# Block products for the mixer's projections, with their weight blocks prepared during the first gate/up

## The chip, the cores and the metric

The kernel runs on one core of a Trainium2 chip. The core has five engines that each take their own instructions in order: PE (TensorE, matmul), DVE (VectorE), ACT (ScalarE), POOL (GpSimd) and SP (SyncE), the last of which only issues transfers here. The metric is the time of the program on the device in microseconds, over one block of the network with T = 1024 tokens and D = 1024.

## The reference

One encoder block in float32, three residual steps with layer norms. FF is 4096, there are 8 attention heads of width 64, and the recurrent part has 512 channels.

```python
x = layer_norm(DN_ALPHA * x + 0.5 * swiglu(x, ffn1_w_gate, ffn1_w_up, ffn1_w_down), ln1_g, ln1_b)
z = x @ w_in                        # columns: q, k, v, lx, lg (512 each), 8 forget gates
fox = forgetting_attention(q, k, v, fg)
u = causal_depthwise_conv(lx, conv_w, conv_b)
lru = gelu(lg) * rg_lru(u, ...)     # h_t = a_t h_{t-1} + sqrt(1 - a_t^2) (i_t u_t)
x = layer_norm(DN_ALPHA * x + concat(fox, lru) @ w_out, ln2_g, ln2_b)
x = layer_norm(DN_ALPHA * x + 0.5 * swiglu(x, ffn2_w_gate, ffn2_w_up, ffn2_w_down), ln3_g, ln3_b)
# swiglu(x, wg, wu, wd) = (silu(x @ wg) * (x @ wu)) @ wd
```

## The kernel before

**Precision.** Every float32 product is three matmuls in the format fp32r (`mm3`, L163 to L165): each operand is split into a high part (a cast on ACT) and a low part (a subtraction on DVE), and high x high, low x high and high x low are accumulated.

**Stages.** The kernel goes through gate/up 1 (to about 630 us), down 1 (to 919), the mixer's projections (to about 1183), the attention and W_out (to about 1370), gate/up 2 (to 1985) and down 2. At each seam the next stage's first operands need DVE and ACT.

**Block products.** gate/up and down multiply 2 x 2 block matrices with seven block products instead of eight (Strassen's scheme). In gate/up each of 16 pairs of column groups has two matrices, gate and up, and for each the products `one, two, six, five, seven, three, four` of 12 matmuls of 128x512. Their weights are sums and differences of four blocks of the weight, called 11, t1, 22, t2, 21, t4, t3. Normally DVE forms and splits these as it goes (L344 and others); the copies and additions of the products' results are done by ACT and DVE between.

**Prepared weights.** For the first pair of gate/up 2 these seven operands are made ahead, during gate/up 1. `prepare` is a generator: at each step it casts, splits and stores one block of weights (`keep`, L277, L278, store to the DRAM tile `pre_d` at L282), with a difference (`less`, L285) between. The blocks come over SP into two buffers called `aux`. A quarter job is one half of the rows of one matrix: six loads of 128 KB, seven keeps of 256 KB, four differences. There are four of them (2 matrices x 2 halves), 28 keeps in all. In gate/up 1 one step is taken for each matrix of pairs 1 to 15, behind product `two`. What the loop leaves over is drained by a bare loop after it. The keeps take their buffers from the pool `gu_ws`, whose space down 1 uses again for its own splits.

**Projections.** Before the mixer, x1 (the output of the first norm) is transposed and split into `xT`. For each of four groups of 128 columns, lx and lg, then q and k, are plain products: 8 blocks of x by 8 of w for each half of the tokens, 4 x 24 = 96 matmuls of 128x512 for two matrices. Their weights are loaded (`columns`) and split (`split_ws`) on the way. After groups 1 and 3 come eight tiles of v each (matmuls of 128x256). Convolution, gates and recurrence (`lru`) follow each half of lx and lg on ACT, DVE and POOL. q, k and v go to DRAM through POOL, and the attention loads them for each head over SP (`q`, `kh`, `kl`, `cum`, `v`).

**Order.** A scheduler orders each engine's instructions at build time, from the order of the code and from what each instruction waits for. `issue_after` keeps an instruction behind another one. On the chip each engine then takes its list strictly in order.

Of the kernel before, what the change touches and what calls it, by code (L numbers as in the profile page):

```python
# [9 lines left out]
F32 = mybir.dt.float32  # L10
# [7 lines left out]
P = 128  # L18
# [34 lines left out]
OPERANDS = "11", "t1", "22", "t2", "21", "t4", "t3"  # L53

# [5 lines left out]
class Block:  # L60
# [115 lines left out]
    def to_xT(self, i, in_s):  # L176

        nc = self.nc
        cols = slice((i % 4) * P, (i % 4 + 1) * P)
# [6 lines left out]
        self.scale_acc(i)  # L186
# [33 lines left out]
    def down_tile(self, i, f_tiles, scale, halves=(0, 1)):  # L220

        ts = slice(i * P, (i + 1) * P)
        for d in halves:
# [4 lines left out]
            self.nc.vector.scalar_tensor_tensor(self.acc[i][:, ds], pa, scale, self.acc[i][:, ds], op0=ALU.mult, op1=ALU.add)  # L228

# [32 lines left out]
    def prepare(self, views, to_d, wsp, ap):  # L262

        nc, v = self.nc, self.nc.vector

        def raw():
            return ap.tile([P, 2, P], F32, tag="aux", name=self.nm("aux"))

        def load(view, k, c):
            t = raw()  # L270
            nc.sync.dma_start(t, view[:, k:k + 2, c * P:(c + 1) * P])
            return t

        def halves(src):
            t = wsp.tile([P, 4, P], F32R, tag="ws", name=self.nm("ws"))
            hi, lo = t[:, 0:2, :], t[:, 2:4, :]
            nc.scalar.copy(hi, src)  # L277
            v.tensor_tensor(lo, src, f32(hi), ALU.subtract)  # L278
            return t

        def keep(m, h, n, src):
            nc.gpsimd.dma_start(to_d[m, OPERANDS.index(n), h], f32(halves(src)))  # L282

# [3 lines left out]
        for m, view in enumerate(views):  # L287
            for h in range(2):
                up, down = 2 * h, 4 + 2 * h
                a, b = load(view, up, 0), load(view, up, 1)  # L290
                yield
                keep(m, h, "11", a)
                less(b, a)
                a = load(view, down, 1)
                yield
                keep(m, h, "t1", b)
                yield
                keep(m, h, "22", a)
                less(a, b)
                b = load(view, down, 0)  # L300
                yield
                keep(m, h, "t2", a)
                yield
                keep(m, h, "21", b)
                less(b, a)
                a = load(view, down, 1)
                yield
                keep(m, h, "t4", b)
                b = load(view, up, 1)
                yield  # L310
                less(a, b)
                keep(m, h, "t3", a)
# [15 lines left out]
    def gate_up(self, wg, wu, h_d, rows, bank, tp, wsp, raws=None, later=None, aside=None, ready=None, steps=None):  # L328
# [211 lines left out]
        def ready_pair(g, u):  # L540
# [7 lines left out]
            def fetch(n, m, to):  # L548
                for l in range(2):
                    nc.sync.dma_start(f32(to[l]).rearrange("p (h k) f -> p h k f", h=2),  # L550
                                      ready[both.index(m), OPERANDS.index(n)].rearrange("h p (l k) f -> l p h k f", l=2)[l])
# [125 lines left out]
        for pair in range(FF // P // 2):  # L677
# [39 lines left out]
            for m in (gate, up):  # L717
# [18 lines left out]
    def down_ffn(self, wd, h_d, ln, order, vp, wp, finish, src, hooks, tail, homes, after=None):  # L736
# [6 lines left out]
        with self.pool("dn_gb") as gp, self.pool("dn_b") as bp, self.pool("dn_t", 2) as tp:  # L743
# [55 lines left out]
            def norm(i):  # L799
                self.layer_norm(i)  # L800

# [116 lines left out]
    def lru(self, c, half, s, tp, mix, state, between):  # L918

        nc, v = self.nc, self.nc.vector  # L920

        def tmp(tag, shape=(P, H), dt=F32):
            return tp.tile(list(shape), dt, tag=tag, name=self.nm(tag))

        zx = tp.tile([P, H + LINE], F32, tag="zx", name=self.nm("zx"))[:, 0:H + 3]
        if half == 0:
            v.memset(zx[:, 0:3], 0.0)
        else:
            v.tensor_copy(zx[:, 0:3], state["z"])
        nc.scalar.copy(zx[:, 3:], s[:, 0, :])  # L930
        if half == 0:
            state["z"] = self.small.tile([P, 3], F32, tag="zc", name=self.nm("zc"))
            v.tensor_copy(state["z"], zx[:, H:H + 3])
# [6 lines left out]
        v.tensor_tensor(ul, u, f32(uh), ALU.subtract)  # L940
        g = tmp("g")
        nc.scalar.activation(g, s[:, 1, :], AF.Square)
        nc.gpsimd.tensor_scalar(g, g, 0.044715, 1.0, op0=ALU.mult, op1=ALU.add)
        v.tensor_tensor(g, g, s[:, 1, :], ALU.mult)
        nc.scalar.activation(g, g, AF.Tanh, scale=GELU_C)
        v.scalar_tensor_tensor(g, g, 1.0, s[:, 1, :], op0=ALU.add, op1=ALU.mult)
        between()
# [19 lines left out]
        if half == 0:  # L967
            state["h"] = self.small.tile([P, 1], F32, tag="hc", name=self.nm("hc"))
            v.tensor_copy(state["h"], e[:, H - 1:H])
        v.scalar_tensor_tensor(g, g, -0.5, e, op0=ALU.mult, op1=ALU.mult)  # L970
        hs = slice(half * H, (half + 1) * H)
        nc.scalar.copy(mix[0][:, hs], g)
        v.tensor_tensor(mix[1][:, hs], g, f32(mix[0][:, hs]), ALU.subtract)
# [23 lines left out]
    def columns(self, w_in, *offs):  # L997

        r = self.raw([P, 2, KT, P])
        for n, off in enumerate(offs):  # L1000
            self.nc.sync.dma_start(r[:, n], w_in.rearrange("(k p) f -> p k f", p=P)[:, :, off:off + P])
        return [self.split_ws(r[:, n], KT) for n in range(2)]

    def mixer_in(self, w_in, lw, qw, later):

        nc = self.nc
        wv = w_in.rearrange("(k p) f -> p k f", p=P)
        self.q_d, self.k_d = (self.dram.tile([HEADS // 2, 2, P, T], F32, name=f"{n}_d") for n in "qk")
        self.v_d = self.dram.tile([HEADS, T, P], F32, name="v_d")
        self.mix_lru = []  # L1010

        with self.tc.tile_pool(name="lru_t", bufs=1, reuse_waits="tile") as tp, \
                self.tc.tile_pool(name="lru_g", bufs=4, reuse_waits="tile") as gp, \
                self.tc.tile_pool(name="ev", bufs=3, reuse_waits="tile") as ev:
            def lru_half(c, half):
                s = self.s_tile()
                self.project(s[:, 0, :], lw[0], half)
                self.project(s[:, 1, :], lw[1], half)
                for g in later[:2]:
                    g()  # L1020
                self.lru(c, half, s, tp, mix, state, lambda: qk_half(c, half))

            def qk_half(c, half):
                s = self.s_tile()
                hs = slice(half * H, (half + 1) * H)
                for n in range(2):
                    self.project(s[:, n, :], qw[n], half)
                for g in later[2:]:
                    g()
                later.clear()  # L1030
                for n, (scale, dst) in enumerate(zip((-0.125, 1.0), (self.q_d, self.k_d))):
                    hl = [ev.tile([P, H], F32R, tag="ev", name=self.nm("ev")) for _ in range(2)]
                    nc.scalar.activation(hl[0], s[:, n, :], AF.Copy, scale=scale)
                    nc.vector.scalar_tensor_tensor(hl[1], s[:, n, :], scale, f32(hl[0]), op0=ALU.mult, op1=ALU.subtract)
                    for l in range(2):
                        nc.gpsimd.dma_start(dst[c, l, :, hs], f32(hl[l]))

            def v_tile(i):
# [3 lines left out]
                for k in range(KT):  # L1042
                    wh, wl = (w[:, k % 4, :] for w in vw[k // 4])
# [359 lines left out]
```

## Time and profile before

| what | value |
|---|---|
| median of 3 runs | 2316.66 us (2316.2 to 2316.94) |
| the profiled execution | 2315.55 us, span 2313.8 us, mean granted clock 0.998 |
| PE busy | 2295.7 us, 99% of the span |
| DVE busy | 1634.9 us, 71% |
| ACT busy | 1017.2 us, 44% |
| POOL busy | 214.2 us, 9% |
| DMA | 314.67 MB, mean 136 GB/s |

Times in the rows are microseconds unless marked ns. A group of instructions is told as line, engine, operation, result <- inputs, shape and count, then busy time and mean ns of one, then the engine's idle time ahead of them with what ended it. Matmuls overlap: one lasts 0.39 us, but the next starts after a fraction of that.

### The profile page before, as it was taken

To read this page: it belongs to the slowest core of one execution; us is meant where nothing else is said; L and a number is where in the kernel's file an instruction comes from. 1 tells how busy PE (TensorE), PEld (TensorE's weight loads), DVE (VectorE), ACT (ScalarE), POOL (GpSimd) and SP (SyncE) were. 2 spreads that over 40 slices of the span, in tenths; PEclk is the share of its full clock that TensorE was granted. 3 is DMA by queue.
4 is the path that set the end of the run, shared out by engine and by line. 5 is a ranking of instruction groups with operands and counts; after the bars stand their busy time and mean duration, and the time that the engine had idled before them with its cause. 6 is when DMAs were issued, how large, how long until landed. Compare 5 with 4: busy or idle time off the path is not lost.

```text
span 2313.8 us, 28429 instructions
## 1 busy us (share of the span) xinstructions
PE 2295.7 (99%) x10705; PEld 1912.3 (83%) x10705; DVE 1634.9 (71%) x2509; ACT 1017.2 (44%) x1611; POOL 214.2 (9%) x369
## 2 busy tenths in 40 slices
PE   9999999999999999999999999999999999999998
PEld 7888888888888888888898888888888888888887
DVE  8766666666577788866667999565656566577886
ACT  5444434344344345453556855333333333344341
POOL 0121010101000000111133200000000000000000
PEclk9999999999999999999999999999999999999999
DMA  4333333333375443132275834232323232564541
GB/s 150 135 115 139 110 135 112 137 107 141 117 272 209 146 146 108 60 101 101 96 222 130 256 117 145 91 124 91 120 86 119 87 119 87 202 245 162 183 144 73
DMA packets 190249, 314.67 MB, mean 136 GB/s; under 512 B 9424, under 2 KB 113168, under 8 KB 190112
## 3 DMA queue, kind: packets, MB, share of 16 engines
q1 hardware_dynamic: 164800, 226.55, 30.3%
q0 software_dynamic: 25312, 86.31, 9.5%
q8 instruction: 84, 1.38, 0.2%
q14 instruction: 53, 0.43, 0.1%
HBM read 222.61 MB, written 90.21 MB: 135 GB/s over the span
## 4 chain that ended last, share of the span: by engine, by line
PE 94%; DVE 3%; ACT 1%; issue 1%; DMA 0%; SPq 0%; DVEq 0%; ACTq 0%
PE x L163 10%; PE x L165 10%; PE x L164 10%; PE b L163 8%; PE b L164 8%; PE b L165 8%; PE s L165 6%; PE s L164 6%; PE s L163 6%; PE a L163 6%; PE a L164 6%; PE a L165 6%; PE a L1188 1%; PE a L1167 1%; PE a L1045 1%; PE a L1047 1%
## 5 line engine op out<-in xcount | busy, mean ns | idle before, releaser
L343 ACT CAST ws<-t 128x512 fp32r<-128x512 f32 x240 | 149.1, 623 | 387.7 <-PE b L164 265.2
L343 ACT CAST ws<-raw 128x512 fp32r<-128x512 f32 x180 | 111.9, 623 | 248.7 <-PE x L164 243.1
L344 DVE TENSOR_TENSOR ws<-raw,ws 128x512 fp32r<-128x512 f32 x180 | 123.9, 689 | 127.2 <-ACT ws L343 114.8
L344 DVE TENSOR_TENSOR ws<-t,ws 128x512 fp32r<-128x512 f32 x240 | 164.7, 687 | 63.1 <-ACT ws L343 61.2
L164 PE MATMUL a<-ws,ws 128*128 128x512 f32 x512 | 199.7, 390 | 0.2
L163 PE MATMUL a<-ws,ws 128*128 128x512 f32 x512 | 199.3, 390 | 0.4 <-ACT row L667 0.4
L163 PE MATMUL b<-As,ws 128*128 128x512 f32 x512 | 199.4, 389 | 0.2 <-ACT row L658 0.2
L164 PE MATMUL b<-As,ws 128*128 128x512 f32 x512 | 199.3, 389 | 0.0
L165 PE MATMUL b<-As,ws 128*128 128x512 f32 x512 | 199.2, 389 | 0.0
L165 PE MATMUL a<-ws,ws 128*128 128x512 f32 x512 | 199.2, 389 | 0.0
L163 PE MATMUL x<-As,ws 128*128 128x512 f32 x504 | 196.2, 389 | 0.0
L164 PE MATMUL x<-As,ws 128*128 128x512 f32 x504 | 196.1, 389 | 0.0
L165 PE MATMUL x<-As,ws 128*128 128x512 f32 x504 | 196.1, 389 | 0.0
L163 PE MATMUL x<-A,ws 128*128 128x512 f32 x496 | 193.3, 390 | 0.1
L165 PE MATMUL x<-A,ws 128*128 128x512 f32 x496 | 193.1, 389 | 0.0
L164 PE MATMUL x<-A,ws 128*128 128x512 f32 x496 | 193.0, 389 | 0.0
L768 ACT CAST ws<-raw 128x1024 fp32r<-128x1024 f32 x112 | 117.4, 1050 | 159.2 <-PE a L164 88.2
L771 DVE TENSOR_TENSOR ws<-raw,ws 128x1024 fp32r<-128x1024 f32 x112 | 136.7, 1221 | 50.9 <-ACT ws L768 50.3
L697 POOL DMA_DIRECT2D h_d<-row x96 | 68.8, 719 | 969.1 <-DVE row L691 964.6
L163 PE MATMUL s<-ws,ws 128*128 128x512 f32 x384 | 149.5, 389 | 0.0
L165 PE MATMUL s<-ws,ws 128*128 128x512 f32 x384 | 149.4, 389 | 0.0
L164 PE MATMUL s<-ws,ws 128*128 128x512 f32 x384 | 149.4, 389 | 0.0
(290 smaller groups left out, 5231.9 us busy)
## 6 DMA issues: line engine op xcount, KB each, us to landing
raw<-h_d SPq DMA_DIRECT2D x56, 1024.0 KB, 5.4
h_d<-row POOLq DMA_DIRECT2D x96, 512.0 KB, 3.4
wd<-in_ffn_w_down_dram SPq DMA_DIRECT2D x32, 1024.0 KB, 7.6
raw<-in_ffn_w_gate_dram SPq DMA_DIRECT2D x30, 1024.0 KB, 5.3
raw<-in_ffn_w_up_dram SPq DMA_DIRECT2D x30, 1024.0 KB, 5.3
h_d<-row POOLq DMA_DIRECT2D x32, 256.0 KB, 2.4
raw<-in_w_in_dram SPq DMA_DIRECT2D x16, 512.0 KB, 4.9
pre_d<-ws POOLq DMA_DIRECT2D x28, 256.0 KB, 2.6
```

The lines of the kernel that those rows point to most:

```text
L163: mm(out, ah, bh, start=first, stop=False, skip_group_check=goes_on)
L164: mm(out, ah, bl, start=False, stop=False, skip_group_check=goes_on)
L165: mm(out, al, bh, start=False, stop=last, skip_group_check=goes_on)
L343: nc.scalar.copy(hi, src)
L344: v.tensor_tensor(lo, src, f32(hi), ALU.subtract)
L697: nc.gpsimd.dma_start(d[:, 2 * n:2 * n + 2], t.rearrange("p (r t) -> p r t", r=2))
L768: cast = nc.scalar.copy(hi, src)
L771: self.mark = v.tensor_tensor(lo, src, f32(hi), ALU.subtract)
L1045: nc.tensor.matmul(pa[:, 0:width], xh, wh[:, 0:width], start=k == 0, stop=False)
L1047: nc.tensor.matmul(pa[:, 0:width], xl, wh[:, 0:width], start=False, stop=k == KT - 1)
L1167: nc.tensor.transpose(pa[:, (j % 4) * P:(j % 4 + 1) * P], p[:, j * P:(j + 1) * P], self.ident)
L1188: mm(pv[:, ps], vt[:, j, :], pts[h, qt][j // 4][l][:, j % 4, ps], start=j == 0 and l == 0, stop=j == last and l == 1)
```

## The change

lx with lg, and q with k, of each column group become one unit: the 2 x 2 block matrix of tokens by two column blocks, with seven products of 12 matmuls (84 instead of 96). The operands of x for it (`s1` to `s4`) are formed and split by DVE and ACT from x1's rows ahead of the units, and the first 16 tiles of work in the mixer are now the v tiles. Since x1's rows are overwritten by those sums, they are stored to DRAM (`x1_d`) and loaded again in the attention.

The weights' seven operands for the eight units, and v's split, are no longer made in the mixer: `prepare` makes them in gate/up 1 and keeps them in DRAM (`wq_d`, `wv_d`). Its list is now 16 single blocks for v, 16 quarter jobs for the units, and the four quarter jobs for gate/up 2, in this order. A step is taken three times for each matrix instead of once. The `aux` buffers become four and are filled ahead; `gu_ws` has 15 buffers instead of 16.

The core of the diff:

```diff
     def prepare(self, jobs, wsp, ap):
+        specs = iter([src for blocks, _ in jobs for src in blocks])
+        ready = []
+        def fetch():                       # the next block over SP into an aux buffer
+            src = next(specs, None)
+            if src is not None:
+                t = ap.tile([P, 2 * P], F32, tag="aux", name=self.nm("aux"))
+                t = t.rearrange("p (k f) -> p k f", f=src.shape[-1])
+                nc.sync.dma_start(t, src)
+                ready.append(t)
         def keep(to, src):
...
             nc.scalar.copy(hi, src)
             v.tensor_tensor(lo, src, f32(hi), ALU.subtract)
-            nc.gpsimd.dma_start(to_d[m, OPERANDS.index(n), h], f32(halves(src)))
+            nc.gpsimd.dma_start(to, f32(t).rearrange("p l k f -> p l (k f)"))
...
+        for _ in range(4):
+            fetch()
+        yield
+        for blocks, to in jobs:
+            if len(blocks) == 1:           # v
+                keep(to, ready[0])
+                drop()                     # and fetch the next
+                yield
+                continue
+            a, b = ready[0:2]
+            keep(to["11"], a)
+            less(b, a)
+            drop()
+            yield
+            keep(to["t1"], b)
+            yield
...
 # gate_up, for each matrix of pairs 1 to 15
                 for step in ("two", "six", "five", "seven", "three"):
                     getattr(m, step)()
-                    if steps and step == "two":
+                    if steps and step in ("two", "five", "three"):
                         with self.tc.issue_after(self.weight_load.ins):
                             next(steps, None)
...
 # the kernel's body
-            blk.pool("gu_ws", 16) as wsp, blk.pool("aux", 2) as ap, blk.banks() as bank, ExitStack() as inner:
+            blk.pool("gu_ws", 15) as wsp, blk.pool("aux", 4) as ap, blk.banks() as bank, ExitStack() as inner:
...
-        steps = blk.prepare(blk.gu_views(ffn2_w_gate[0], ffn2_w_up[0]), pre_d, wsp, ap)
+        jobs = blk.mixer_jobs(w_in[0])
+        for m, view in enumerate(blk.gu_views(ffn2_w_gate[0], ffn2_w_up[0])):
+            jobs += blk.quarter_jobs(view, (0, P), lambda n, h: pre_d[m, OPERANDS.index(n)][:, :, h])
+        steps = blk.prepare(jobs, wsp, ap)
         finish = blk.gate_up(ffn1_w_gate[0], ffn1_w_up[0], h_d[0], rows, bank, tp, wsp, raws, open_s4, lambda: blk.mixer_consts(
...
         for _ in steps:
             pass
...
 # the mixer: one unit (lx with lg, or q with k)
+            def product(x, name, new=True):
+                w = w_ops.pop(0)
+                fetch_w()                  # the operand three products ahead, from wq_d over SP
+                for k in range(4):
+                    self.mm3(x, (w[:, 0, k, :], w[:, 1, k, :]), x_op(name, k), new and k == 0, k == 3, not new)
+            def unit(c0, c1, c3, then):
...
+                product(total, "11")
+                nc.scalar.copy(c0, total)
+                two = self.a_tile()
+                product(two, "12")
+                v.tensor_tensor(c0, two, c0, ALU.add)
+                product(total, "s2", False)
+                nc.scalar.copy(c1, total)
+                product(z, "s1")
+                nc.scalar.copy(c3, z)
+                product(total, "s3", False)
+                v.tensor_tensor(c3, total, c3, ALU.add)
+                product(z, "s4", False)
+                v.tensor_tensor(c1, z, c1, ALU.add)
+                product(total, "22", False)
+                then[7](total)
```

Between these calls `unit` runs the work that hangs on a finished part: convolution, gates, the stores of q and k, the splits of `s4` in the first unit, W_out's rows in the last.

**DVE at the end of gate/up 1.** Before, its list goes from the last pair's weight splits (L344), the last step (L278) and the combinations after products two, seven and three of the last matrix (L651, L661, L664) straight on to the splits of down 1's first operands (L771):

```order
L664 TENSOR_TENSOR row_4822<-b_4973,row_4823 128x512
L344 TENSOR_TENSOR ws_4900<-t_4897,ws_4899 128x512
L278 TENSOR_TENSOR ws_4956<-aux_4664,ws_4956 128x256
L651 TENSOR_TENSOR row_4824<-b_5042,row_4825 128x512
L771 TENSOR_TENSOR ws_5168<-raw_5155,ws_5167 128x1024
L661 TENSOR_TENSOR row_4825<-x_5013,row_4824 128x512
L664 TENSOR_TENSOR row_4825<-b_5069,row_4823 128x512
L771 TENSOR_TENSOR ws_5172<-wd_5157,ws_5171 128x1024
```

After, with the line numbers moved (steps are L283 and L287, the combinations L693, L703 and L706, down 1's splits L813), the beginning and the end of what stands there:

```order
L703 TENSOR_TENSOR row_5179<-x_5384,row_5178 128x512
L287 TENSOR_TENSOR aux_5533<-aux_5533,aux_5526 128x256
L283 TENSOR_TENSOR ws_5555<-aux_5533,ws_5555 128x256
L283 TENSOR_TENSOR ws_5559<-aux_5535,ws_5559 128x256
L287 TENSOR_TENSOR aux_5535<-aux_5535,aux_5533 128x256
L706 TENSOR_TENSOR row_5179<-b_5447,row_5177 128x512
L283 TENSOR_TENSOR ws_5566<-aux_5535,ws_5566 128x256
L287 TENSOR_TENSOR aux_5542<-aux_5542,aux_5553 128x256
```

```order
L283 TENSOR_TENSOR ws_5916<-aux_5887,ws_5916 128x256
L287 TENSOR_TENSOR aux_5894<-aux_5894,aux_5905 128x256
L283 TENSOR_TENSOR ws_5921<-aux_5894,ws_5921 128x256
L813 TENSOR_TENSOR ws_5971<-raw_5958,ws_5970 128x1024
L813 TENSOR_TENSOR ws_5975<-wd_5960,ws_5974 128x1024
```

Between the two pieces stand only L283 and L287: from behind L706 to L813 there are 91 rows of steps, 58 of L283 and 33 of L287. With those among the last pair's own rows, 69 of L283 and 39 of L287 lie between the last L693 and the first L813. On ACT the casts of the same steps (L282) stand ahead of down 1's first cast (L810).

**SP at the beginning of the attention.** `raw` are W_out's rows for the heads, `q`, `kh`, `kl`, `cum` and `v` are head 0's operands. Before, these loads follow the last load of the projections' weights (v's second half, L1081):

```order
L1081 DMA raw_9168<-in_w_in_dram 128x8x256
L1106 DMA raw_9434<-in_w_out_dram 128x2x1024
L1106 DMA raw_9444<-in_w_out_dram 128x2x1024
L1106 DMA raw_11160<-in_w_out_dram 128x2x1024
L1127 DMA q_9471<-q_d 64x1024
L1128 DMA kh_9472<-k_d 64x1024
L1129 DMA kl_9473<-k_d 64x1024
```

After, they follow the last two operands of the last q/k unit, a row of x1, and two loads of W_out's rows:

```order
L1130 DMA wq_10201<-wq_d 128x1024
L1130 DMA wq_10216<-wq_d 128x1024
L1396 DMA row_10326<-x_d 128x1024
L1273 DMA raw_12030<-in_w_out_dram 128x2x1024
L1273 DMA raw_12166<-in_w_out_dram 128x2x1024
L1291 DMA q_10330<-q_d 64x1024
L1292 DMA kh_10331<-k_d 64x1024
L1293 DMA kl_10332<-k_d 64x1024
```

The v tiles, which in the order of before stand on PE between the last q/k products and the attention's first scores, are at the mixer's beginning now; between the last unit and the first scores PE has only pieces of W_out.

More of the change, by code (lines that the diff above doesn't have):

```diff
@@ L916, in gate_w, with conv @@
         return self.split(raw, [P, 2, P], tp, "gw")
-    def lru(self, c, half, s, tp, mix, state, between):
+    def conv(self, c, zx, tmp):
         nc, v = self.nc, self.nc.vector
[L922 to L933, printed above, removed]
         u = tmp("u")
@@ L1014, in mixer_in, with tmp, v_weights, v_tile @@
                 self.tc.tile_pool(name="ev", bufs=3, reuse_waits="tile") as ev:
[L1015 to L1038, printed above, removed]
+            def tmp(tag, shape=(P, H), dt=F32):
+                return tp.tile(list(shape), dt, tag=tag, name=self.nm(tag))
+            def v_weights(cc, k):
+                if cc == 0:
+                    return tuple(t[:, k % 4, :] for t in vw[k // 4])
+                return tuple(t[:, k, :] for t in v1)
+            def v_tile(cc, i):
                 pa = self.a_tile()
@@ new lines, in parts @@
+            def parts(name, j, src):
+                js = slice(j * P, (j + 1) * P)
+                for hi, lo, x in zip(*(t if isinstance(t, list) else [t] for t in ops[name]), (src[:, 0:2], src[:, 2:4]) if isinstance(ops[name][0], list) else (src,)):
+                    self.cast = nc.scalar.copy(hi[:, :, js], x)
+                    last = v.tensor_tensor(lo[:, :, js], x, f32(hi[:, :, js]), ALU.subtract)
+                    if name == "s1" and j == 0:
+                        self.rest = last
@@ new lines, in fetch_w @@
+            def fetch_w():
+                at = next(loads, None)
+                if at is not None:
+                    t = self.wsp.tile([P, 4 * VW], F32R, tag="ws", name=self.nm("wq"))[:, 0:8 * P]
+                    self.row_load = nc.sync.dma_start(f32(t), self.wq_d[at].rearrange("p l h f -> p (l h f)"))
+                    if at[0] == 0 and at[1] < 3:
+                        self.issue_behind(self.row_load, self.rest)
+                    w_ops.append(t.rearrange("p (l k f) -> p l k f", l=2, f=P))
```

384 lines of the change are left out of this document (260 added, 124 removed).

## The prediction

> **What bounds the kernel now.** I read the busy shares first, then the chain that ended last, the table of windows, and the groups by form. The first fence holds the page's line of busy times, its chain by engine, and windows (columns: length, busy time and count of PE, PE's weight loads, DVE, ACT, POOL, then granted clock, DMA share, GB/s): gate/up 1 at rest, its last 40 us, the first 10 us of down 1, the mixer's projections, the attention.
>
> ```profile
> PE 2295.7 (99%) x10705; PEld 1912.3 (83%) x10705; DVE 1634.9 (71%) x2509; ACT 1017.2 (44%) x1611; POOL 214.2 (9%) x369
> ...
> PE 94%; DVE 3%; ACT 1%; issue 1%; DMA 0%; SPq 0%; DVEq 0%; ACTq 0%
> 0.00:58.00 58.00, 53.97 (x273) 44.82 (x274) 48.55 (x80) 34.81 (x60) 0.69 (x6) 0.97 0.42 150
> 400.00:470.00 70.00, 70.00 (x310) 57.96 (x310) 47.16 (x73) 28.08 (x48) 7.67 (x12) 1.00 0.38 134
> 590.00:630.00 40.00, 40.00 (x178) 33.14 (x177) 18.63 (x26) 13.53 (x21) 3.29 (x5) 1.00 0.36 133
> 630.00:640.00 10.00, 9.55 (x43) 7.58 (x42) 7.64 (x9) 4.48 (x5) 0.92 (x2) 1.00 0.77 274
> 919.00:1183.00 264.00, 263.04 (x1362) 224.65 (x1361) 180.09 (x330) 124.86 (x197) 43.27 (x69) 1.00 0.34 107
> 1183.00:1370.00 187.00, 182.98 (x1121) 157.89 (x1120) 156.89 (x388) 126.27 (x289) 54.99 (x117) 1.00 0.60 173
> ```
>
> PE bounds every stage: it is never idle in 400 to 470 us and idle 0.96 us of 264 in the projections. A matmul taken away is therefore worth its whole slot, and any wait that reaches PE is paid in full. The next view, PE's timeline where gate/up 1 ends, gives the slot (starts 0.226 to 0.227 us apart; over the window, 70/310 = 0.226) and the price of that seam today: 0.84 us from 630.56 to 631.39.
>
> ```profile
> 629.65 0.39 PE L165 MATMUL x<-A,ws 128*128 128x512 f32 x1
> 629.88 0.39 PE L163 MATMUL x<-A,ws 128*128 128x512 f32 x1
> 630.10 0.39 PE L164 MATMUL x<-A,ws 128*128 128x512 f32 x1
> 630.33 0.39 PE L165 MATMUL x<-A,ws 128*128 128x512 f32 x1
> 630.56 0.39 PE L163 MATMUL a<-ws,ws 128*128 128x512 f32 x1
> 631.39 0.73 PE L163 MATMUL a<-ws,ws 128*128 128x512 f32 x2 [0.45 <-ACT row L667]
> ```
>
> **Step 1, PE's work.** For each of the eight units (lx with lg, and q with k, four column groups each) seven products of 12 matmuls replace 96 matmuls of 128x512: 12 fewer each, 96 in all, and the order of PE has exactly 96 rows fewer. 96 x 0.2267 = **-21.8 us**. Nothing else on PE changes in number.
>
> **Step 2, the steps left over at the end of gate/up 1.** Here I expect the change to be decided. The generator of steps grows from 4 quarter jobs of 7 steps to 20, with 16 single blocks of v ahead: 1 + 16 + 140 = 157 steps. The loop over pairs takes three for each matrix, 15 x 2 x 3 = 90. So 67 are issued by the bare loop behind gate/up, and DVE's and ACT's orders show them ahead of the first operands of down 1: behind the combination after product two of the last up (row 742) stand 110 rows of DVE before L813's first, 69 of them splits (L283), 39 differences (L287). DVE and ACT work in order, so PE cannot begin down 1 before these are through. The durations are those of the same operations before: cast, difference, split, and the loads and stores that go with them.
>
> ```profile
> L277 ACT CAST ws<-aux 128x256 fp32r<-128x256 f32 x28 | 11.4, 406 | 13.7 <-PE x L164 11.5 <-DVE aux L285 2.0
> L285 DVE TENSOR_TENSOR aux<-aux,aux 128x256 f32<-128x256 f32 x16 | 6.8, 424 | 11.0 <-DMA aux<-in_ffn_w_up_dram 6.5 <-DMA aux<-in_ffn_w_gate_dram 4.3
> L278 DVE TENSOR_TENSOR ws<-aux,ws 128x256 fp32r<-128x256 f32 x28 | 11.9, 425 | 18.3 <-ACT ws L277 18.3
> L771 DVE TENSOR_TENSOR ws<-raw,ws 128x1024 fp32r<-128x1024 f32 x112 | 136.7, 1221 | 50.9 <-ACT ws L768 50.3
> L768 ACT CAST ws<-raw 128x1024 fp32r<-128x1024 f32 x112 | 117.4, 1050 | 159.2 <-PE a L164 88.2 <-PE s L164 60.5 <-issue 5.2
> ...
> DMA to landing us min/median/max: 2.1/2.7/7.2
> pre_d<-ws POOLq DMA_DIRECT2D x28, 256.0 KB, 2.6
> ```
>
> Let E be the end of PE's work in gate/up 1; product two of the last up ends five products earlier, at E - 5 x 12 x 0.227 = E - 13.6. Three paces are possible for a job of 7 splits and 4 differences:
> - DVE alone: 11 x 0.425 = 4.7 us. That is a floor only, since the differences chain: each of the four differences waits for the one before, and its cast and split follow it.
> - The chain difference, cast, split (0.424 + 0.406 + 0.425 = 1.26), four times, and three more splits of which one or two come beside it: with the handoffs I estimate 6.5 us when every block has landed. The four buffers of 128x256 are refilled as they fall free, so some loads are waited for; by the landing times in the fence (2.1 to 2.7 us, and more under load) I make it 7.4 to 8.4 us.
> - The DMA: a job loads 6 x 128 KB and stores 7 x 256 KB, 2.62 MB. From E - 13.6 on that is 69 stores and some 53 loads, 25 MB, and the first three 1 MB loads of down 1 fall among them: 28 MB. The busiest window above moved 274 GB/s at a share of 0.77, hence 356 at a full share: 79 to 103 us, of which the 15 buffers behind the stores take two jobs off DVE's shoulders.
>
> 9.86 jobs at 6.5 us are 64 us, at 8.4 us 83, by the DMA 79 to 103. Then come the landing of a last store that holds a buffer of down 1 (2.6, partly beside), one cast (1.05) and two splits of 1.22 before PE starts, some 3.7 us. I take 84 us for the jobs, near the upper chain and the lower DMA price since both press there: PE starts again at E - 13.6 + 84 + 3.7 = **E + 74**; the ends are E + 54 and E + 93. The Trainium skill, DMA: Bandwidth & Descriptors, Specifications, puts the HBM side at about 358 GB/s for a core; the trace's 0.77 share of 274 agrees, and by the page's figure alone the 28 MB take an estimated 78 us, so the gap would be E + 69.
>
> What would hide it: nothing. PE's first work in down 1 is L163 on the operands of L813. The loads of down 1's third slot stand behind all loads of steps on SP, and add to the wait rather than cover it.
>
> **Step 3, the last pair.** The copies of products six and five on ACT and the additions seven and three on DVE stand among step rows; a bank that is read late holds the next product. At 0.41 us a row and one to four rows ahead this is 0 to 3 us; I take **+1.5**.
>
> **Step 4, the clock.** The first window above, with PE's start after idling in it, was granted 0.97: 0.03 x 58 = 1.7 us lost. A gap of 70 us should cost the same: **+1.7**. The Trainium skill, TensorE: Matmul & The Clock Gate, Part 1, says that after an idle window of about 3.4 us PE runs at half clock for the next one; half of 3.4 is an estimated 1.7 us, and the row agrees.
>
> **Step 5, the 90 steps in the loop** (more casts, splits and stores per pair). DVE is busy 47.16 of 70 us; six steps a pair bring some 4 us in each 38.1 (168 slots), against 0.8 before. It stays under 80%, and matmuls do not wait: **0**. If the cover goes, PE waits for a split of a weight block, at most 1 to 2 us a pair, which I leave to the range.
>
> **Step 6, the mixer.** The 16 v tiles now come first, while DVE does the last norms, the transposes' splits and the sums of x blocks; the fifth v tile wants its bank back about when DVE has finished norm 7. 0 to 8 us, **+3**. In the units DVE loses its weight splits of 128x1024 (20 x 1.22 = 24.4) and gains the combinations of products; the prepared blocks are fetched three products ahead (3 x 2.72 us). DVE was busy 180.09 of 264 us, so (180.09 - 24.4) / 4 = 39 for a column group, of which I put some 7 (v tiles, transposes) ahead of the units: 32 us beside 2 x 84 + 12 slots of PE, 40.8 us. 0 to 6 us, **+1.5**.
>
> **Step 7, the seam to the attention.** Before, head 0's q, kh and kl were issued from 1164.77 while PE still had v tiles, so they lay hidden:
>
> ```profile
> 1164.77 0.47 SPq L1127 DMA_DIRECT2D q<-q_d  x1
> ...
> 1168.52 1.53 SPq L1129 DMA_DIRECT2D kl<-k_d  x1
> 1177.36 0.62 PE L1146 MATMUL s<-kh,q 128*128 128x512 f32 x2
> q<-q_d SPq DMA_DIRECT2D x16, 256.0 KB, 6.0
> kl<-k_d SPq DMA_DIRECT2D x16, 256.0 KB, 7.0
> ```
>
> Now the v tiles are done long ago, and these loads stand on SP behind two 1 MB loads of w_out that wait for buffers which the last q/k unit and the last gating release. The last k half leaves PE two products before the end; its store and load (2.6 and 6 to 7 us) follow, and PE has about 5.7 us of W_out pieces to cover. 3 to 12 us, **+8**.
>
> **Sum:** -21.8 + 74 + 1.5 + 1.7 + 0 + 3 + 1.5 + 8 = +67.9. The profiled execution took 2315.55 us (span 2313.8 and 1.75 around it), 1.1 under the median of 2316.66. 2315.55 + 67.9 = 2383.4, I say **2383**. With all low ends (-21.8 + 54 + 1.7 + 3) it is +37, 2352; with all high ends (-21.8 + 93 + 3 + 1.7 + 8 + 6 + 12) +102, 2418.
>
> **Rivals.**
> - The steps are no bound, faster. If DVE got through the leftover rows without holding down 1 (they would have to be done, or stand behind L813), only steps 1, 6 and 7 would count: -21.8 + 12.5 to -21.8 + 3, 2297 to 2306. It decides if the leftovers cost under 21.8 - 4 = 18 us, that is under 0.3 us for each of 108 rows from E - 13.6 on. Against it: each takes 0.425 by the groups above, and DVE keeps its order. 4 in 100.
> - The chain alone: loads and stores keep up and a job takes 6.5 to 7 us. PE starts at E + 54 to E + 59, total 2352 to 2366. For it: the stores of before landed in 2.6 us beside full work. 25 in 100.
> - The DMA is the bound and every load is late: 95 us or more for the jobs, E + 85 and beyond, total 2395 to 2420. For it: stores now write 1 KB runs, and 512-byte reads run beside them. 20 in 100. The Trainium skill, SBUF — State Buffer, SBUF: two separate sides, warns that certain DVE operations keep GpSimd from writing descriptors; if differences of two SBUF tiles did so, stores would be late and this case would hold.
> - The gain is not realised in the mixer, because DVE (32 of 40.8 us) and ACT evacuate late: 10 to 20 us on top, 2393 to 2403. 8 in 100.
> - No change within 0.2% (4.6 us, about what a measurement of this kernel can tell): several of these would have to cancel. 2 in 100.
>
> The forecast has the remaining 41. Slower in all cases but the first and the last: 94. The range 2350 to 2412 leaves out the faster case and the far ends.
>
> **What would show it.** In the changed profile: one idle stretch of PE of about 74 us at about 630, ended by DVE at L813, with DVE at L283 and L287 and ACT at L282 through all of it; DMA at 240 to 300 GB/s there. 96 fewer matmuls; gate/up 1 otherwise as long as before; the projections about 20 us shorter less some stalls; a gap before the first L1312. I am wrong if PE does not stop at 630, or stops under 20 us: then DVE ran these rows earlier than its order seems to allow, or in far less than 0.42 us each.

## The result, and the profile after

The changed kernel takes 2426.82 us (median of 4 runs, 2422.41 to 2433.25) against 2316.54: a ratio of 1.0478, 95% interval 1.0454 to 1.0502. It is slower by 110 us, where the forecast's sum was 67.9; the sign and the place were right, the size lies 15 us above the range. The profiled execution took 2425.57 us, its span is 2423.9.

The page of the changed kernel, its line of busy times and the chain; then windows, with the columns of the prediction's first fence: gate/up 1 at rest, its last 13 us, and the 86 us behind it.

```profile
PE 2290.4 (94%) x10609; PEld 1897.6 (78%) x10609; DVE 1720.0 (71%) x2745; ACT 1064.9 (44%) x1767; POOL 311.1 (13%) x505
...
PE 63%; DVE 2%; issue 2%; DMA 2%; ACT 2%; SPq 0%; POOL 0%; DVEq 0%; ACTq 0%; POOLq 0%
```

```profile
100.00:600.00 500.00, 495.74 (x2175) 408.64 (x2174) 351.76 (x591) 217.15 (x393) 98.73 (x147) 1.00 0.48 161
627.00:640.00 13.00, 11.72 (x52) 9.37 (x52) 7.38 (x19) 4.60 (x13) 6.78 (x10) 1.00 0.89 292
640.00:726.00 86.00, 1.01 (x5) 0.51 (x3) 38.53 (x93) 23.99 (x60) 41.17 (x60) 0.53 0.88 294
```

PE was 99% busy and is 94%: its busy sum is 5 us smaller, the span 110 us longer. In the last window it does nothing, DVE works less than half of the time (38.5 of 86 us), and the transfers are at a share of 0.88. PE's timeline shows both ends of that stop:

```profile
640.62 0.39 PE L167 MATMUL x<-A,ws 128*128 128x512 f32 x1
726.30 1.28 PE L165 MATMUL a<-ws,ws 128*128 128x512 f32 x2 [85.29 <-ACT ws L810]
```

From 640.62 to 726.30 are 85.7 us, for a distance of 0.23 before. Where the 110 us went, by the starts of the first and last matmuls of each stage in PE's timelines of the two kernels:

| stretch | before | after | difference |
|---|---|---|---|
| to the last matmul of gate/up 1 | 630.33 | 640.62 | +10.3 |
| from there to the first of down 1 | 0.23 | 85.68 | +85.5 |
| down 1 | 309.98 | 310.47 | +0.5 |
| mixer, to the last before the scores | 236.70 | 237.62 | +0.9 |
| from there to the first scores | 0.12 | 13.67 | +13.5 |
| attention, to the first product of gate/up 2 | 209.16 | 209.09 | -0.1 |
| the rest | 927.33 | 926.71 | -0.6 |

By these starts, down 1 of the kernel before ends at 940.5 us and its projections at 1177.2; the 919 and 1183 given with the stages above are rougher.

The mixer's +0.9 is -21.8 for the 96 matmuls, +5.4 for 24 matmuls of W_out that now stand ahead of the scores instead of behind them, and 17.3 us that are left over, most of them waits (shown below). The attention has those 24 fewer and is no shorter: it lost 5.3 us more. Some 2 of these are lost by the matmuls right behind the stop, up to ten of which start 0.43 us apart instead of 0.23, and 1.8 are more waits of PE; the remainder isn't traced.

These figures are from one profiled execution of each kernel. Where the same code ran in other runs below, gate/up 1 with 90 steps lost 8.0 to 10.6 us, and the stop ahead of the scores was 12.6 to 16.5 us.

The waits of all engines from 627 to 727 us (us in total, times, longest) and the landing times of the steps' loads there:

```profile
ACT ws L282 <- DVE aux L287: 45.4, 29, 5.7
DVE ws L283 <- ACT ws L282: 33.7, 53, 1.9
POOL wq_d L284 <- DVE ws L283: 31.4, 30, 5.4
DVE aux L287 <- DMA aux<-in_w_in_dram: 10.2, 6, 4.7
DVE ws L813 <- DMA pre_d<-ws: 1.5, 1, 1.5
```

```profile
DMA to landing us min/median/max: 2.2/3.7/7.2
```

Cast, split and difference wait for each other in a ring, as in the second pace of the forecast, and the ring waits for loads: 25 of the 55 were awaited, 30.3 us in all. Their median time to landing rose from 2.7 to 3.7 us; the longest is 7.2 as before. The last row is the store that holds down 1's buffer.

PE's own waits: two rows from gate/up 1, then the largest from the projections up to the scores:

```profile
PE b L165 <- ACT row L700: 3.6, 4, 2.2
PE x L165 <- DVE row L703: 1.3, 1, 1.3
```

```profile
PE s L1312 <- DMA kh<-k_d: 13.3, 1, 13.3
PE s L165 <- ACT raw L1157: 5.4, 8, 0.7
PE s L165 <- ACT raw L1160: 2.8, 4, 0.7
PE a L166 <- DVE w L158: 1.8, 2, 1.1
```

The twelve waits for L1157 and L1160 show on PE's timeline as a start 1.06 us after the last instead of 0.23:

```profile
1161.87 0.39 PE L167 MATMUL s<-As,wq 128*128 128x512 f32 x1
1162.93 0.50 PE L165 MATMUL s<-As,wq 128*128 128x512 f32 x1 [0.68 <-ACT raw L1157]
```

### The profile page after: what moved, and what is told of

Same layout as the page of the kernel before. It is cut to its first block, busy times and chain, and to the rows that moved or that the text cites. A ratio compares the mean times of both kernels' runs of the same rounds, so it can differ in the third digit from the quotient of the medians.

```text
span 2423.9 us, 29536 instructions
## 1 busy us (share of the span) xinstructions
PE 2290.4 (94%) x10609; PEld 1897.6 (78%) x10609; DVE 1720.0 (71%) x2745; ACT 1064.9 (44%) x1767; POOL 311.1 (13%) x505
## 4 chain that ended last, share of the span: by engine, by line
PE 63%; DVE 2%; issue 2%; DMA 2%; ACT 2%; SPq 0%; POOL 0%; DVEq 0%; ACTq 0%; POOLq 0%
PE a L166 6%; PE a L167 6%; PE a L165 6%; PE s L165 5%; PE x L167 5%; PE x L165 5%; PE x L166 5%; PE s L167 5%; PE s L166 5%; PE b L167 4%; PE b L166 4%; PE b L165 4%; PE a L1354 1%; DMA kh<-k_d 1%; PE a L1333 1%
## 5 line engine op out<-in xcount | busy, mean ns | idle before, releaser
L165 PE MATMUL a<-ws,ws 128*128 128x512 f32 x512 | 200.0, 391 | 85.3 <-ACT ws L810 85.3
L810 ACT CAST ws<-raw 128x1024 fp32r<-128x1024 f32 x112 | 117.5, 1050 | 163.5 <-PE a L166 83.0
L165 PEld LDWEIGHTS a<-ws,ws 128*128 128x128 f32 x512 | 96.5, 188 | 106.0 <-ACT ws L810 85.7
L813 DVE TENSOR_TENSOR ws<-raw,ws 128x1024 fp32r<-128x1024 f32 x112 | 136.6, 1220 | 51.4 <-ACT ws L810 49.5
L165 PE MATMUL s<-ws,ws 128*128 128x512 f32 x384 | 149.5, 389 | 0.0
L167 PE MATMUL s<-ws,ws 128*128 128x512 f32 x384 | 149.4, 389 | 0.0
```

The source lines that it names most:

```text
L165: mm(out, ah, bh, start=first, stop=False, skip_group_check=goes_on)
L167: mm(out, al, bh, start=False, stop=last, skip_group_check=goes_on)
L810: cast = nc.scalar.copy(hi, src)
L813: self.mark = v.tensor_tensor(lo, src, f32(hi), ALU.subtract)
```

## The experiments

Theory A is that of the forecast: the stop is the steps that the loop leaves over. The rivals were that the steps cost PE the same wherever they stand (B), and that down 1's own first loads set the stop (C). Inside the stop, the loads' waits (L) stood against the rate of the transfers (D). Runs without a ratio are single executions; since the changed kernel's own four executions lie 11 us apart, they are read by their stages and not by their totals.

### The steps spread over six places

```diff
                 m.one()
+                if steps:
+                    with self.tc.issue_after(self.weight_load.ins):
+                        next(steps, None)
...
-                    if steps and step in ("two", "five", "three"):
+                    if steps and step in ("two", "six", "five", "seven", "three"):
```

> The changed kernel with a step after each of six products of every matrix (one, two, six, five, seven, three: 180 places for 157 steps), so that nothing is left for the bare loop. Theory A (the stop of PE before down 1 is the leftover steps in the lists of DVE and ACT): the stop falls from 85.5 us to about 1, the stalls inside gate/up 1 grow with the steps from 10.3 to about 10.3 x 157/90 = 18, total 2425.6 - 84.5 + 7.7 = about 2349. Rival B (the steps need time that PE waits for wherever they stand, by DVE, ACT or the transfers): the stalls inside gate/up 1 grow by what the stop loses, total about 2400 to 2430.

Measured: 2352.41 us, ratio to before 1.0153 (1.0136 to 1.0170). PE's timeline at the seam, and PE's waits in gate/up 1:

```profile
657.50 0.39 PE L167 MATMUL x<-A,ws 128*128 128x512 f32 x1
657.73 0.39 PE L165 MATMUL a<-ws,ws 128*128 128x512 f32 x1
```

```profile
PE x L167 <- DVE ws L386: 6.2, 8, 1.7
PE x L165 <- ACT row L696: 3.7, 2, 2.1
PE x L165 <- ACT row L690: 2.7, 1, 2.7
```

The stop is gone whole, 85 us of it, so A holds, and B falls: where the stop lost 85 us, gate/up 1 grew by only 16.9. Still, it now ends at 657.5, 27.2 us later than before the change instead of the 18 expected: the cost in the loop grows faster than the number of steps.

### One step for each matrix

```diff
-                    if steps and step in ("two", "five", "three"):
+                    if steps and step == "two":
```

> The changed kernel with one step for each matrix, as before the change: 30 places, 127 steps left over instead of 67. Theory A at the 1.28 us that a leftover step cost (85.5/67): the stop grows by 60 x 1.28 = 77 to about 162 us, the stalls inside gate/up 1 fall from 10.3 to 1 or 2, total about 2493. Rival C (the stop is set by the first loads of down 1, which wait on SP's queue and for the transfers, not by the number of steps): it stays at some 85, total about 2417.

Measured: 2496.15 us, and on PE's timeline

```profile
792.06 1.28 PE L165 MATMUL a<-ws,ws 128*128 128x512 f32 x2 [159.61 <-ACT ws L810]
```

127 leftover steps stop PE for 160 us, 67 for 85.5: 1.26 and 1.28 us a step. The stop goes with the number of steps, so C falls. Gate/up 1 ends at 632.06, so 30 steps in the loop cost 1.7 us, 90 cost 10.3, 157 cost 27.2. This run has the same 15 weight buffers as the changed kernel, so the buffer taken away costs at most 1.7 us by itself.

### Eight buffers for the loads

```diff
-            blk.pool("gu_ws", 15) as wsp, blk.pool("aux", 4) as ap, ...
+            blk.pool("gu_ws", 13) as wsp, blk.pool("aux", 8) as ap, ...
...
-        for _ in range(4):
+        for _ in range(8):
             fetch()
```

> The changed kernel with eight aux buffers filled ahead instead of four (and 13 weight buffers instead of 15, to have the space). Theory L (a leftover job takes 9.8 us instead of the chain's 6.9 because its loads are awaited): jobs at about 6.9, 9.86 x 6.9 = 68 us from 13.6 before the end of gate/up 1, the stop falls to about 58, total about 2398. Rival D (28 MB at the 290 GB/s that the transfers move is the limit): the stop stays at 80 to 86, total 2420 to 2427.

Measured: 2414.05 us; PE's timeline, and the window of the stop:

```profile
711.81 1.28 PE L165 MATMUL a<-ws,ws 128*128 128x512 f32 x2 [71.59 <-ACT ws L810]
```

```profile
640.00:711.00 71.00, 0.22 (x1) 0.00 (x0) 35.67 (x93) 21.13 (x60) 41.11 (x59) 0.52 0.99 357
```

The stop shrinks from 85.3 to 71.6, between L and D. With loads further ahead the transfers run at a share of 0.99 and 357 GB/s, so for these bytes there is hardly more to gain: the 14 us were awaited loads, the 71.6 left are the bytes. The forecast had 356 GB/s for a full share, and its lower price by the transfers comes to E + 69 (79 - 13.6 + 3.7). The Trainium skill, DMA: Bandwidth & Descriptors, Specifications, gives about 358 GB/s for a core's HBM side; this window agrees.

A second thing: the loop's own loss is gone too. From 100 to 600 us, with the same 90 steps, PE makes as many matmuls as before the change (2207; the changed kernel 2175) and is never idle:

```profile
100.00:600.00 500.00, 500.00 (x2207) 413.81 (x2206) 356.02 (x601) 220.94 (x396) 98.76 (x147) 1.00 0.48 162
```

The two other executions with four buffers and 90 steps, in the next two experiments, made 2185 and 2187. So in the changed kernel the loss between these marks came from awaited loads. About 7 us came at the start instead (PE waits of 2.6 for L427 and 1.2 for L421); some 4 of them lie ahead of the first load of a step, at 52.65 us, so those belong to the 13 weight buffers and not to the loads.

### The second accumulator in its own tile

```diff
-                total, z = s[:, 0, :], s[:, 1, :]
+                total, z = s[:, 0, :], self.a_tile()
```

> The changed kernel with the unit's second accumulator z in a PSUM tile of its own instead of the second half of the tile that holds the first. Theory Z (PE's twelve waits of 0.83 us for ACT's copies L1157 and L1160 come from the two accumulators' sharing one tile, so that a product into one waits for the copy out of the other): the waits go, the projections are 10 us shorter, total about 2415. Rival: the copies are awaited for the products' own sake, or DVE's combinations are awaited instead: 0 to 3 us, total 2422 to 2426.

Measured: 2410.12 us. PE's waits from the v tiles to the scores:

```profile
PE s L1312 <- DMA kh<-k_d: 8.0, 1, 8.0
PE a L166 <- DVE ue L971: 2.0, 5, 0.8
PE a L165 <- ACT ua L970: 1.8, 4, 0.6
```

All twelve waits are gone and the projections are 10.2 us shorter (237.62 to 227.38). `total` and `z` were two halves of one tile, and a product into one half waited for the copy out of the other, though the data are apart. What was not expected: the wait at the scores fell too, from 13.3 to 8.0. Waits for the convolution (L970, L971), 3.8 us, have come up in their place.

### W_out's loads behind head 0's

```diff
-            self.nc.sync.dma_start(r, wv[:, f0:f0 + 2, :])
+            with self.tc.issue_after(self.row_load.ins):
+                self.nc.sync.dma_start(r, wv[:, f0:f0 + 2, :])
```

> The changed kernel with the two 1 MB loads of W_out's rows issued behind head 0's loads instead of ahead of them (nothing else). Theory S (PE's 13.4 us before the first scores are head 0's 128 and 256 KB loads queueing in the transfers behind those 2 MB): by the 5 to 7 us that 2 MB take at 290 to 360 GB/s the stop shrinks, to about 6 to 8 us, total about 2419. Rival (the loads wait for the last stores of q and k or for space, not for the transfers): the stop stays at 12 to 14, total 2422 to 2428.

Measured: 2415.26 us. The transfers that SP issues in the changed kernel, SP's longest wait there, then the transfers in this one, and PE's first scores in this one:

```profile
1270.01 1.77 SPq L1273 DMA_DIRECT2D raw<-in_w_out_dram  x2
1271.89 0.80 SPq L1291 DMA_DIRECT2D q<-q_d  x1
1272.79 0.55 SPq L1292 DMA_DIRECT2D kh<-k_d  x1
```

```profile
SPq L1273 <- DVE mix L1018: 16.7, 1, 16.7
```

```profile
1259.00 0.47 SPq L1292 DMA_DIRECT2D q<-q_d  x1
1261.34 0.45 SPq L1293 DMA_DIRECT2D kh<-k_d  x1
```

```profile
1271.94 0.40 PE L167 MATMUL a<-w,mix 128*128 128x512 f32 x1
1272.18 0.39 PE L1313 MATMUL s<-kh,q 128*128 128x512 f32 x1
```

The stop falls to nothing, more than theory S: it was not only the 2 MB in the transfers, but also SP's queue that held head 0's loads. Ahead of them stood two loads that wait for buffers, the first of them 16.7 us for the last gating (L1018). Without those two, q is issued 12.9 us earlier, 2 of them because the whole mixer runs that much earlier here. The rival falls. Of the 13.4 us the program kept some 8, since the attention became 5.5 us longer (214.66 against 209.09).

### The edits together, and what gate/up 1 still lost

First all of them, with six aux buffers and 14 weight buffers, or with eight and 13:

> The changed kernel with the steps in six places of every matrix, z in its own PSUM tile, W_out's loads behind head 0's, and six aux buffers with 14 weight buffers. By the sum of the single edits: 2352 (steps spread) - 15 (z; the stop before the attention shrank with it) - 6 (loads) = 2331; and if the 27 us of stalls inside gate/up 1 with spread steps come from loads of blocks that are awaited (four buffers), a part of them goes, some 10 us: about 2321. Rival (those stalls come from DVE's and ACT's lists being fuller, whatever the loads): gate/up 1 ends at 657 again, total about 2331. Faster than before only if nearly all of the 27 us go.

> As the one before with eight aux buffers and 13 weight buffers. With four places and eight buffers the stalls after 80 us had gone, and 7 us had come at the start (24 to 78 us). If awaited loads are the cause of the stalls of spread steps, gate/up 1 ends at about 640, total about 2314; if 13 weight buffers are too few for the weights' run ahead, stalls at the weights' splits grow and it is 2325 or more.

Measured: 2328.51 us, ratio 1.0045 (1.0031 to 1.0059), gate/up 1 ends at 648.9; and 2341.61, where it ends at 661.5. The first is 2.5 under the sum of single edits and 7.5 over the hope: six loads ahead took 8.6 of the 27 us, with one weight buffer fewer. The second, where gate/up 1 is 12.6 us longer again, falls to the other case of its expectation, that 13 weight buffers are too few: 7.1 us of these come in the first 80 us, as in the other run with 13. Whether the weight buffers or the eight loads cost the other 5.5 us is not separated.

Then each step was cut: cast now, split, difference and next load at the next step (here as a sketch of `keep`):

```diff
             nc.scalar.copy(hi, src)
-            v.tensor_tensor(lo, src, f32(hi), ALU.subtract)
-            nc.gpsimd.dma_start(to, ...)
+            def split():
+                v.tensor_tensor(lo, src, f32(hi), ALU.subtract)
+                nc.gpsimd.dma_start(to, ...)
+            later.append(split)            # run when the next step begins
```

> The kernel with all four edits (steps in six places, z in its own tile, W_out's loads behind head 0's, six aux buffers and 14 weight buffers), and each step cut in two: the cast stays where it was, the split, the difference and the next load move to the beginning of the following step, so that DVE does not wait in its list for the cast it has just asked for. Theory O (the 18.6 us that gate/up 1 still loses are DVE's and ACT's in-order lists waiting on each other inside a step, which makes the weight splits behind them late): most of it goes, gate/up 1 ends at 632 to 640, total 2310 to 2320. Rival F (DVE's list is simply fuller: 156 splits and 80 differences, 100 us, beside copies that PE awaits): gate/up 1 ends at 645 to 652 again, total 2324 to 2331.

Measured: 2322.95 us, ratio 1.0037 (1.0022 to 1.0051); gate/up 1 ends at 642.9. That lies between the two theories: 6.0 us of the 18.6 were the lists waiting inside a step, where theory O had hoped for most of them. Nearly half of the 12.6 us left came from one place; ACT's timeline there, and PE's:

```profile
161.35 0.20 ACT L926 ACTIVATE lp<-vecs 128x4 f32<-128x4 f32 x1 [5.59 <-DMA vecs<-in_lru_lambda_dram]
161.58 1.28 ACT L927 ACT_TABLE_LOAD   x1
...
163.49 0.58 ACT L706 COPY row<-x 128x512 f32<-128x512 f32 x1
```

```profile
164.12 0.79 PE L165 MATMUL x<-As,ws 128*128 128x512 f32 x1 [3.43 <-ACT row L706]
```

A constant of 2 KB is loaded on POOL's queue, which now also carries the steps' stores; ACT stands 5.6 us for it, and PE's bank is read late. The eleven next starts of PE are 0.43 us apart instead of 0.23, so that the place costs 6 us. So the steps were left out of the two matrices in which the constants are loaded, and last the gates were moved one product later:

```diff
+                here = steps and (pair, m is up) not in ((2, True), (3, False))
...
-                then = {2: [first_conv], 4: [lambda: gates(0)], 6: ...
+                then = {2: [first_conv], 5: [lambda: gates(0)], 6: ...
```

> The kernel with all edits and the split cut off, without steps in two matrices (up of pair 2, gate of pair 3), where small constants are loaded on POOL's queue and ACT waited 5.6 us for one of them; 168 places remain for the 158 steps. Theory P (the 3.6 us stop at 164 us and the half clock behind it, 6 us in all, come from that load standing behind steps' stores on POOL): the stop goes, gate/up 1 ends 4 to 7 us sooner, at 636 to 639, total 2315 to 2318. Rival (the load is late by itself; before the change ACT waited 3.1 us for it): gate/up 1 ends at 642 to 643 as it did, total about 2322.

> As the one before, with the gates' matmuls of each unit one product later (places 5 and 3 instead of 4 and 2), since PE waited for the convolution's split there, five times some 1.2 us in all for the two waits. If those waits are plain lateness of ACT's and DVE's convolution, one product (2.7 us) covers them: the projections shrink by 4 to 6 us, total 2310 to 2314, faster than before the change by 0.1 to 0.3%. Rival (the recurrence behind the gates becomes late, and with it the last gating and the first W_out pieces): no gain or a loss of a few us before the attention, total 2315 to 2320.

Measured without the steps there: 2318.52 us, gate/up 1 ends at 637.3, 5.6 us sooner, and ACT no longer waits for the constant: P holds. With the gates later as well: 2313.95 us against 2315.75, ratio 0.9989 (0.9980 to 0.9998), 11 runs against 15. The projections became 2.2 us shorter by it (227.8 to 225.6), not the 4 to 6 expected; another 2.2 us went in the attention, and nothing here shows why. This last version is far below the changed kernel, and 0.1% below the one before, which is less than the 0.2% that the forecast called telling. Its waits of PE in the projections:

```profile
PE s L1333 <- DMA kh<-k_d: 2.6, 1, 2.6
PE a L166 <- DVE ue L991: 1.6, 3, 0.5
PE s L165 <- ACT zx L1170: 0.7, 1, 0.7
PE s L165 <- ACT raw L1177: 0.7, 1, 0.7
```

Where the 21.8 us go in it: gate/up 1 is 6.9 us longer than before (637.19 against 630.33), the seam to down 1 costs 1.1 more, the mixer to its last matmul is 11.1 shorter (225.64 against 236.70, with the 5.4 us of W_out in it), the scores start 2.8 later, the attention is as long as before (209.54) though its 24 matmuls are gone.

## Why the prediction was right and wrong

- **Step 1** (-21.8): right. 96 matmuls are gone (10705 to 10609). How much of their slots can be kept is another matter: in the last version the mixer, without W_out's 5.4 us, is 16.5 us shorter, and the other 5.3 are lost there.
- **Step 2** (+74, bounds 54 to 93): right in mechanism, shown by the steps in six places and by those in one; 11.5 us short. The price of a job was set at 84/9.86 = 8.5 us, between chain and transfers; it was 9.8 (from 627, where product two of the last up ended, to 723.8, the last split). I priced each pace alone and took a value near the upper end of the chain (83) and the lower end of the transfers (79), as if the two ran side by side. They added up in part: loads that share the transfers with stores landed later, and the chain waited for 25 of 55. With the waits mostly gone the stop was 14 us shorter.
- **Steps 3 and 5** (+1.5 and 0): the step that failed first. Gate/up 1 lost 10.3 us. I took DVE's share (under 80%) for cover, set step 5 to nothing, and had no upper end for it in the sum. DVE did stay at 70% (351.76 of 500 us), and PE waited all the same. What counts in the loop is that a step's rows stand in the in-order lists between a bank's copy and a weight's cast and split, and each may wait for a load or a store. The timelines of DVE, ACT and PE at one such place, and of ACT and PE at the dearest one:

```profile
165.06 0.42 DVE L287 TENSOR_TENSOR aux<-aux,aux 128x256 f32<-128x256 f32 x1 [2.87 <-DMA aux<-in_w_in_dram]
168.84 1.14 ACT L385 CAST ws<-t 128x512 fp32r<-128x512 f32 x2 [3.09 <-DMA wv_d<-ws]
169.89 0.58 ACT L700 COPY row<-b 128x512 f32<-128x512 f32 x1
170.51 0.50 PE L165 MATMUL b<-As,ws 128*128 128x512 f32 x1 [0.89 <-ACT row L700]
...
399.33 0.62 ACT L385 CAST ws<-t 128x512 fp32r<-128x512 f32 x1 [3.99 <-DMA wq_d<-ws]
402.06 0.79 PE L165 MATMUL b<-As,ws 128*128 128x512 f32 x1 [2.19 <-ACT row L700]
```

  At the first place a difference waits for its load, the steps' stores go out late, a weight cast waits for such a store to give its buffer back, the copy behind that cast is late, and PE with it. At the second, with the slow matmuls behind it, PE lost 4.0 of the 10.3 us. The run with eight buffers filled ahead shows what came first in the changed kernel: with it PE lost nothing from 100 to 600 us, although the pool that weights and steps share was two buffers smaller. With the steps spread, 27.2 us, the causes are more: six loads ahead took 8.6 us, the cut inside a step 6.0, and the two matrices left out for the constants 5.6; the last 7 us stay open. A pool of its own for the steps wasn't tried.
- **Step 4** (+1.7): the clock did fall (0.53 over the stop, and the first matmuls behind it start up to 0.43 us apart). The first twelve matmuls of down 1 took 4.7 us instead of 3.5, but down 1 as a whole lost only 0.5; some of its first operands were awaited in the same microseconds. The rule of the Trainium skill, TensorE: Matmul & The Clock Gate, Part 1, is borne out in the granted clock. The price was smaller here; behind the stop ahead of the scores, for which I had put nothing, it was some 2 us.
- **Step 6** (+4.5): failed, 17.3 us. The part I doubted, the v tiles ahead, cost next to nothing (50.4 us with their transposes, 50.0 before). In the units I weighed DVE's load and never asked what a product into an accumulator waits for; 10 of the 17 were the shared tile, and 1.8 are two waits for W_out's splits (L158).
- **Step 7** (+8, bounds 3 to 12): the queue that I named, but 13.4 us, shown by moving the two loads. I also had the last store and load of k in mind, whereas head 0 needs q and k of the first column group, stored long before. And I did not price the 24 matmuls of W_out that moved ahead of the scores: the attention without them still took its 209 us, so their 5.4 us bought nothing there.

In sum the terms came out at 110.0 instead of 67.9: 11.5 from step 2, 8.8 from 3 and 5, 12.8 from 6, 10.8 from 7, less 1.2 from 4 and 0.6 elsewhere. Step 2 stayed inside its bounds; with it alone set right the forecast would have been 2395, inside the range. What carried the time out of the range are the terms that left their bounds: the loop's waits (step 5, put at nothing), the accumulators' waits (step 6) and the seam (step 7). Even all high ends together had come to 2418 only. The misses fell to one side because each was a wait, and a wait that one does not see is priced at nothing. Two slips in the working changed nothing: two steps a pair come to 1.3 us of DVE and not 0.8 (step 5), and the window taken for the projections (step 6) also held 21.5 us of down 1. Of the rivals, the chain alone (E + 54 to E + 59) is excluded: even with eight buffers, the transfers full, the stop was 71.6 us. The DMA-bound one (95 us or more for the jobs, E + 85) had the right price for the stop, 97 us from 627 and E + 85.7, but not quite its mechanism: the transfers were at 0.88, and 14 us were waits that earlier loads removed. Whether DVE's differences also held up POOL's stores is not separated by any run; issuing one took POOL 0.69 us in the stop and 0.56 before.

## What to carry to other kernels

Count the places and the steps when work is handed out by a generator: what the loop does not take is paid whole behind it, here at 1.28 us a step, and one loop that takes six instead of three is worth 74 us. A busy share is no cover on an engine that takes its list in order: ask for each inserted instruction what it may wait for, and what stands behind it that the bounding engine needs. Two accumulators that are read and written in turn belong in two tiles, and a load that waits for space does not belong ahead of one that is wanted now.

## What the runs showed of the hardware

- A core's transfers, loads and stores mixed, came to 357 GB/s at a share of 0.99 over 71 us, and 294 at 0.88 when 25 of 55 loads were awaited.
- A store of 256 KB landed in 2.6 us (median) before; in the stop it took 4.2 and 3.3 (the first 41 and the last 28), and a load of 128 KB 3.7 instead of 2.7.
- A short stop of PE inside steady work was followed by half the clock: at 402 us of the changed kernel two matmuls started 2.6 us apart, and from 402 to 405 us the granted clock was 0.50, with starts 0.43 us apart. Behind a distance of 1.28 us, at 170.5 us, it stayed at 1.00.
